# Two blocks of the output projection by seven products instead of eight, with the weight sums made during the attention heads

## The chip, the cores and the metric

The kernel runs on one core of a Trainium2 chip. The metric is the device time in microseconds (us) of one execution. Before the change the median of three runs is 1013.32 us, from 1013.02 to 1014.41.

## The reference

The kernel computes one decoder layer over 256 tokens of width 2048. A normalised input goes through one wide projection; from that come a multi-head latent attention (16 heads) and a short gated convolution; both are projected to the model's width, merged by sigmoid gates, and go through one shared output projection and a last normalisation:

```python
h = _rmsnorm(x, pre_norm_g)
proj = jnp.einsum('bsd,de->bse', h, w_in)
...
y_mla = jnp.einsum('bse,ed->bsd', attn, w_o_mla)
...
y_conv = jnp.einsum('bse,ed->bsd', b_gate * conv * jax.nn.silu(z_conv), w_o_conv)
merged = jax.nn.sigmoid(g_mla) * y_mla + jax.nn.sigmoid(g_conv) * y_conv
out = jnp.einsum('bsd,de->bse', merged, w_out)
x = x + _rmsnorm(out, post_norm_g)
```

All of it is float32. The change concerns `out = merged @ w_out`, with `merged` of 256x2048 and `w_out` of 2048x2048.

## The kernel before

**Products.** A float32 matrix is split into a high part (rounded to the matmul's type) and a low part (the rest), and a product is three matmuls: high by high, low by high, high by low. ACT makes the high part and DVE the low part (`split_act`, L265 and L266). Weights come in *units* of 128x2048 numbers, 1 MB, each loaded by SP into a `raw` buffer of three and split by halves of 1024 columns into `whi` and `wlo`, of which there are five buffers each; so a split waits until PE has let go of the fifth half before it. `plan` lists the units in their order; `take(i)` hands unit i to PE and makes sure that the loads are three units and the splits one unit ahead. A unit stands for 512 features of the contraction and 512 columns. For all 256 tokens (two row blocks, t = 0 and 1) it takes 4 x 2 x 3 = 24 matmuls of 128x512.

**Stages.** After the latent projections 16 heads follow. Head h has four units of a convolution weight (tile `cv`, `channels`), and between them its scores (`sc`, `sw`, made by `score`), the softmax, and the queries and keys of the next group of two heads (`group_a`, whose results are `qn_hi`, `qn_lo` and `kn`; `made[h]` says in which head). `score(h + 1, later=True)` puts a group's first scores right behind the last `cv` matmuls of the head before. In most heads DVE and ACT also make forms of the input (`make_forms`, one step at each `next(form_steps)`, three steps a head), which go out to DRAM through ACT's queue and come back later. Then come the two big projections (tiles `sq` and `sX`, `sY`, `sZ`), which already use the sets of seven products over 2x2 blocks, and then the output stage.

**Output stage.** `merged` stands transposed in four tiles `m_both0` to `m_both3` of 512 features each, with high and low parts, split from `turned_m` (L266 and L265). `w_out` has four blocks c of 512 columns, by four units k. Before the change all four blocks are plain products, 16 units, in the order of `out_order`; each block and row block has a PSUM bank, is squared and summed on ACT (`out_block`, tile `junk`), multiplied with the gain on DVE (`og`, L1503), and finished by `finish` (row block 0) and `finish_by_two` (row block 1): inverse root, scaling and addition of the residual `xr` (L1519), and the stores.

**Order.** The order of PE and of whatever is wrapped in `tc.keep_in_program_order` is that of the program. Everything else is put in order by a scheduler before the kernel is built, which orders each engine's instructions by a timeline of its own. So an added instruction on DVE can change where its neighbours stand. On the chip each engine runs its list in that order, and an instruction that waits holds what is behind it on its engine.

Of the kernel before, what the change touches and what calls it, by code (L numbers as in the profile page):

```python
# [18 lines left out]
P = 128  # L19
# [63 lines left out]
def tile_layer(ctx: ExitStack, tc: tile.TileContext, xw, w0, xb, x, pos, pvec, post_g, wc, wz, wcv, wkr, wqk, wqr, wv, cwr, wsq, out):  # L83
# [61 lines left out]
    out_order = [(0, 0), (0, 1), (1, 0), (1, 1), (0, 2), (1, 2), (0, 3), (1, 3)]  # L145
    out_order += [(c, k) for c in (2, 3) for k in range(4)]
    u_out = {ck: add(wsq[4, ck[0], ck[1]]) for ck in out_order}

    raws, splits, early = {}, {}, {}
    done = {"raw": 0, "split": 0, "end": u_first[1] + 1}  # L150

    def load_raw(i):
        ap, w = plan[i]
        t = early.get(i)
        if t is None:
            t = wpool.tile([P, UNIT], F32, name=f"raw{i}", tag="raw", bufs=3)
        if i == 0:
            pieces = [(S, XW, w0), (XW, 2 * XW, xb[0])]
        elif i in (1, 2):

            pieces = [(j * XW, (j + 1) * XW, xb[2 * i - 1 + j]) for j in range(2)]
        elif i in u_first:
            pieces = []
        else:
            pieces = [(0, w, ap)]
        for a, b, piece in pieces:
            d = nc.sync.dma_start(out=t[:, a:b], in_=piece)
            if i >= u_first[0]:
                tc.keep_in_program_order(d)
        raws[i] = t  # L170
        if i == u_qa[5]:
            tc.keep_in_program_order(nc.sync.dma_start(out=tables_pi, in_=pos))
        if i == u_ckv[1]:
            tc.keep_in_program_order(nc.sync.dma_start(out=x_tok, in_=x))

    def split_unit(i):
# [22 lines left out]
        for h in range(0, w, HALF):  # L199
            n = min(HALF, w - h)  # L200
            if u_out[3, 0] <= i < u_out[3, 3]:
# [6 lines left out]
            split_act(hi[:, :n], lo[:, :n], t[:, h : h + n], i in (u_head[0][1], *u_first, *u_d[0][2][:2]), i in (u_grp["r", 0], u_grp["v", 0], u_head[0][0]))  # L208
            parts.append((hi, lo))
# [13 lines left out]
    def take(i):  # L223
        ahead(i)
        return pieces(splits.pop(i))
# [695 lines left out]

    form, sums = {}, {}
# [8 lines left out]
    form_steps = make_forms()  # L931
# [14 lines left out]
    def turned_unit(far, both, first, tag=None, queue=nc.sync):  # L946
# [4 lines left out]
        def load():  # L951
            name = f"turned_{both.name}{first}"
            if tag:
# [14 lines left out]
        return [[load if i == 0 else None, split(i), None, None] for i in range(len(far))]  # L968
# [25 lines left out]
    for h in range(H):  # L994
# [48 lines left out]
        if h < H - 2:  # L1043
            next(form_steps)
        if v and at == 0 or h == H - 1:
# [22 lines left out]
        if h < H - 2:  # L1068
            next(form_steps)
        channels(h, 2)  # L1070
        if h < H - 2:
            next(form_steps)
        if h == H - 1:
# [51 lines left out]
    LAST = ("f5", "f6", "rb0", "rc0", "rc1", "rb1")  # L1125
# [249 lines left out]
    m_load = [turned_unit(far_m[a:b], m_b, a, tag, nc.gpsimd) for a, b, tag in ((0, 2, "rc0"), (2, 3, "rc1"), (3, 4, "rb1"))]  # L1375
# [91 lines left out]

    m_load[1][0][0]()
# [11 lines left out]
    pss = [[bank(f"out{c}_{t}") for t in range(NT)] for c in range(2)]  # L1480
    for i, (c, kk) in enumerate(out_order[:4]):
        w = take(u_out[c, kk])
        if i == 0:
            last_m[0]()
        elif i == 2:
            m_load[1][0][1]()
        out_products(pss[c], w, kk)
    main.close()


    op = ctx.enter_context(tc.tile_pool(name="op", bufs=1))
    xr = op.tile([P, NT, D], F32, name="xr")
    og = op.tile([P, NT, D], F32, name="og")
    gb = op.tile([P, D], F32, name="gb")
    nc.scalar.dma_start(out=gb[:, :], in_=post_g.to_broadcast([P, D]))

    def out_block(c, t, ps):
# [5 lines left out]
        og_now = nc.vector.tensor_tensor(og[:, t, cs], ps[:, :], gb[:, cs], op=ALU.mult)  # L1503
        if c == 3:
            tc.keep_in_program_order(og_now)
# [50 lines left out]
    for i, (c, kk) in enumerate(out_order[4:6]):  # L1556
        w = take(u_out[c, kk])
        if i == 0:
            last_m[1]()
        out_products(pss[c], w, kk)  # L1560
    tc.keep_in_program_order(nc.sync.dma_start(out=xr[:, :, :], in_=x))
    for c in range(3):
        if c == 2:
            pss.append([bank(f"out{c}_{t}") for t in range(NT)])
        for kk in range(4) if c == 2 else (3,):
            out_products(pss[c], take(u_out[c, kk]), kk)
        for t in range(NT):
            out_block(c, t, pss[c][t])
    nc.vector.reduce_sum(part[:, :], ssq[:, :, :3], axis=mybir.AxisListType.X)
    nc.vector.tensor_scalar(part[:, :], part[:, :], 1.0 / D, EPS, op0=ALU.mult, op1=ALU.add)  # L1570
    pss = [bank(f"out3_{t}") for t in range(NT)]
    for t in range(NT):
        for kk in range(4):
            if t == 0:
                last.append(take(u_out[3, kk]))
            out_products(pss, last[kk], kk, (t,))
        ps = out_block(3, t, pss[t])
# [91 lines left out]
```

## Time and profile before

| what | value |
|---|---|
| median of three runs | 1013.32 us |
| the profiled execution | 1013.55 us |
| its span, first to last instruction | 1011.8 us |
| granted TensorE clock, mean | 0.998 |
| ACT busy / POOL busy | 58% / 17% |
| output stage, first to last of its matmuls | 916.35 to 1003.39 us |
| mean DMA rate over the span | 259 GB/s |

The engines are PE (matmul), PEld (its weight loads), DVE (vector), ACT (scalar), POOL and SP (which here only issues DMAs). The page gives for each the busy time and its share of the span; the chain of work goes back from the last instruction to what released each step; the waits list how long an engine stood idle and on whom it waited. In a timeline a row is start, duration, engine, line, operation, tiles written and read, and in brackets the idle time ahead of it with what ended it. Grouped rows end in the number of instructions, their total and their mean in ns, and the idle time before them. DMA rows give queue, count, size and the median time from issue to landing.

### The profile page before, as it was taken

The numbers are of one execution on the slowest core, as the hardware profiler recorded it, in microseconds if no ns is written. First come the engines' busy times: TensorE is split into PE (matmuls) and PEld (weight loads), VectorE is DVE, ScalarE is ACT, GpSimd is POOL, SyncE is SP. The second block draws the span as 40 slices with busy tenths as digits, with TensorE's granted clock in tenths as the row PEclk, the third lists the DMA queues.
The fourth block names the chain that finished last, engine by engine and source line by source line (L and its number), as shares of the span: only waits on it lengthen the run. The fifth ranks groups of instructions, "written<-read, shape, count | busy, mean of one in ns | idle before, by whom it ended". The sixth has DMA issues, their size and how long they took to land.

```text
span 1011.8 us, 12983 instructions
## 1 busy us (share of the span) xinstructions
PE 1004.2 (99%) x4552; PEld 835.4 (83%) x4552; DVE 811.4 (80%) x1111; ACT 586.3 (58%) x838; POOL 170.7 (17%) x311
## 2 busy tenths in 40 slices
PE   9999999999999999999999999999999999999997
PEld 7888888888888888888888888888888888888886
DVE  7588878868888689877797889898989779997562
ACT  7675656556556456555565465565675664674541
POOL 4620411113211223212133110000000001003000
PEclk9999999999999999999999999999999999999999
DMA  8785768568786668866689779897599989639742
GB/s 338 282 291 183 260 201 304 197 214 276 234 303 232 228 229 283 272 219 232 216 264 338 292 306 291 344 375 218 187 333 296 305 321 260 239 127 322 289 166 84
DMA packets 54369, 261.84 MB, mean 259 GB/s; under 512 B 8768, under 2 KB 13504, under 8 KB 29216
## 3 DMA queue, kind: packets, MB, share of 16 engines
q1 hardware_dynamic: 37728, 214.35, 57.7%
q0 software_dynamic: 12256, 38.13, 14.0%
q10 hardware_dynamic: 4320, 8.54, 2.4%
q8 instruction: 35, 0.57, 0.2%
q14 instruction: 30, 0.25, 0.1%
HBM read 234.80 MB, written 22.02 MB: 254 GB/s over the span
## 4 chain that ended last, share of the span: by engine, by line
PE 98%; DMA 1%; DVE 0%; ACT 0%; SPq 0%; issue 0%
PE cv L88 34%; PE sq L88 17%; PE sX L88 9%; PE z L88 9%; PE out L88 9%; PE sZ L88 4%; PE kn L88 2%; PE qn L88 2%; PE vv L88 2%; PE sY L88 2%; PE ckv L88 2%; PE qa L88 2%; PE qr L88 1%; PE o L88 1%; PE sw L88 1%; DMA raw<-xb_dram 1%
## 5 line engine op out<-in xcount | busy, mean ns | idle before, releaser
L265 ACT ACTIVATE whi<-raw 128x1024 fp32r<-128x1024 f32 (+1 forms) x302 | 306.1, 1028 | 236.7 <-PE cv L88 103.9
L266 DVE TENSOR_TENSOR wlo<-raw,whi 128x1024 fp32r<-128x1024 f32 (+1 forms) x300 | 352.7, 1188 | 101.2 <-ACT whi L265 74.6
L88 PE MATMUL cv<-whi,x_both 128*128 128x512 f32 x1024 | 319.8, 389 | 0.0
L88 PEld LDWEIGHTS cv<-whi,x_both 128*128 128x128 f32 x1024 | 192.3, 188 | 39.5
L88 PE MATMUL cv<-wlo,x_both 128*128 128x512 f32 x512 | 199.5, 390 | 0.0
L88 PEld LDWEIGHTS cv<-wlo,x_both 128*128 128x128 f32 x512 | 96.2, 188 | 19.4
L266 DVE TENSOR_TENSOR slo_V<-b,shi_V 128x1024 fp32r<-128x1024 f32 x60 | 71.5, 1218 | 15.9 <-PE sq L88 8.5
L265 ACT ACTIVATE shi_V<-b 128x1024 fp32r<-128x1024 f32 x60 | 61.5, 1053 | 39.2 <-PE sq L88 21.2
L88 PE MATMUL z<-whi,x_both 128*128 128x512 f32 x256 | 80.0, 389 | 0.0
L366 POOL DMA_DIRECT2D far<-via x64 | 35.4, 559 | 227.2 <-DVE via L358 217.2
L88 PE MATMUL sq<-whi,at_both 128*128 128x512 f32 x256 | 60.6, 389 | 0.0
L88 PE MATMUL sq<-whi,cv_both 128*128 128x512 f32 x256 | 60.6, 389 | 0.0
L88 PEld LDWEIGHTS sq<-whi,cv_both 128*128 128x128 f32 x256 | 48.0, 188 | 10.0
L88 PEld LDWEIGHTS sq<-whi,at_both 128*128 128x128 f32 x256 | 48.0, 188 | 10.0
L88 PEld LDWEIGHTS z<-whi,x_both 128*128 128x128 f32 x256 | 48.1, 188 | 9.9
L88 PE MATMUL z<-wlo,x_both 128*128 128x512 f32 x128 | 49.8, 389 | 0.0
L88 PE MATMUL out<-whi,m_both 128*128 128x512 f32 x208 | 49.4, 389 | 0.0
L88 PE MATMUL sX<-shi_V,form 128*128 128x512 f32 x192 | 47.4, 389 | 0.0
L88 PEld LDWEIGHTS out<-whi,m_both 128*128 128x128 f32 x208 | 39.0, 188 | 8.1
L88 PEld LDWEIGHTS sX<-shi_V,form 128*128 128x128 f32 x192 | 36.0, 188 | 7.5
L265 ACT ACTIVATE shi_Q<-b 128x1024 fp32r<-128x1024 f32 x28 | 28.8, 1052 | 21.5 <-PE sq L88 19.1
L1263 POOL DMA_DIRECT2D b<-wsq_dram x8 | 7.0, 869 | 193.4 <-DVE b L1272 76.8
(304 smaller groups left out, 1568.7 us busy)
## 6 DMA issues: line engine op xcount, KB each, us to landing
raw<-wcv_dram SPq DMA_DIRECT2D x64, 1024.0 KB, 6.2
raw<-wsq_dram SPq DMA_DIRECT2D x48, 1024.0 KB, 7.2
b<-wsq_dram SPq DMA_DIRECT2D x26, 1024.0 KB, 5.7
raw<-wz_dram SPq DMA_DIRECT2D x16, 1024.0 KB, 4.9
raw<-wqk_dram SPq DMA_DIRECT2D x8, 1024.0 KB, 6.8
b<-wsq_dram POOLq DMA_DIRECT2D x8, 1024.0 KB, 11.0
far_form<-form ACTq DMA_DIRECT2D x28, 256.0 KB, 3.3
form<-far_form SPq DMA_DIRECT2D x7, 1024.0 KB, 13.8
```

Of the source, the lines that this page charges most:

```text
L88: return tc.keep_in_program_order(nc.tensor.matmul(*a, **kw))
L265: a = nc.scalar.activation(hi, src, AF.Copy)
L266: b = nc.vector.tensor_tensor(lo, src, hi.bitcast(F32), op=ALU.subtract)
L366: tc.keep_in_program_order(queue.dma_start(out=f[i], in_=m))
L1263: tc.keep_in_program_order(nc.gpsimd.dma_start(out=dst[:, :], in_=wsq[n, c + b, k], accum_op=ALU.add))
```

## The change

Blocks 0 and 3 of the output stay plain. Blocks 1 and 2 are made together: both row blocks of tokens by both halves of the contraction by both blocks of columns are a 2x2 by 2x2 product of blocks, done as seven block products (Q1, V5, V6, V7, V3, V4, Q2) instead of eight. A block product takes one row block of tokens (128) by 1024 features, which is two units of 12 matmuls each. Four of the seven need a sum of weights, and four need a *form* of `merged`, a sum or difference of its blocks.

- **Weight sums.** `make_sums` makes V5, V7, V6 and V4 of the units of blocks 1 and 2: 16 DVE additions of 128x1024, with 16 loads of 512 KB on SP and 16 stores of 512 KB on ACT's queue to `far_sum` in DRAM. They use tiles `at_f` and `cv_f`, whose second halves lie free in the first eight heads. One step is taken at each call of `sums_next(h)`, which stands behind each `next(form_steps)`; seven of the 24 calls, listed in it, do nothing. Only three of the sets need no sum of weights and take their units straight from `wsq`.
- **Forms of merged.** In the output stage `m_form_of` makes V7, V5, V6 and V3: two DVE operations of 128x512 into `m_sums`, a high part on ACT and a low part on DVE over 128x1024. V6 has a negative sign and takes a three-operand instruction for its low part.
- **Banks.** The seven products use three PSUM banks: X for Q1, then V6 on top of it, then V7, then V4; Z for V5, then V3; Y for Q2. In between, the state of a bank is taken out by ACT (`copied`: a from X, c from Z, b from X) and a later one is added by DVE (`added`).
- **Loads.** There are 18 units instead of 16, the splits of all of them are kept in program order, and the loads run five units ahead instead of three. Units of V5, V7 and V4 use a tile `spare` that has room for two and shares its place with `xr`; so the load of `xr` moves to the end of SP's list.
- **The end.** Block 3 has its first two units early in the stage; of its last two, both units of row block 0 come first and then those of row block 1. Before, all four units of row block 1 came behind all four of row block 0.

```diff
+    SUMS = ("V5", "V6", "V7", "V4")
+    far_sum = {(n, u): dram.tile([P, UNIT], F32, name=f"far_sum{n}_{u}") for n in SUMS for u in range(2)}
+    set_raw = {"Q1": (1, 0), "V3": (2, 2), "Q2": (1, 2)}
+    out_order = [(0, 0), (0, 1), (3, 0), ("Q1", 0), ("Q1", 1), (0, 2), ("V5", 0), ("V5", 1), (0, 3), ("V6", 0), ("V6", 1), (3, 1)]
+    out_order += [(n, u) for n in ("V7", "V3", "V4", "Q2") for u in range(2)] + [(3, 2), (3, 3)]
+    in_spare = {u_i: n % 2 for n, u_i in enumerate((6, 7, 12, 13, 16, 17))}
...
-        ahead(i)
+        ahead(i, raw=5 if i >= u_out[0, 0] else 3)
...
+    def make_sums():
+        keep = tc.keep_in_program_order
+        area = [f[:, 4 * i : 4 * i + 4, :].rearrange("p k s -> p (k s)") for f in (at_f, cv_f) for i in (2, 3)]
+        a, b, c, d = area
...
+        bring(0, (0, 1))
+        bring(0, (2,))
+        yield
+        for i in range(4):
+            bring(i, (3,))
+            plus(a, a, b)
+            yield
+            plus(b, b, c)
+            put(i, (1,))
+            yield
+            plus(c, a, c)
+            put(i, (0,))
+            if i < 3:
+                bring(i + 1, (0, 1))
+            yield
+            plus(d, c, d)
+            put(i, (2, 3))
+            if i < 3:
+                bring(i + 1, (2,))
+            yield
...
+    def sums_next(h):
+        q = sum_calls[0] % 3
+        sum_calls[0] += 1
+        if (h, q) not in ((0, 0), (1, 1), (1, 2), (2, 0), (5, 1), (5, 2), (6, 0)):
+            next(sum_steps)
...
+    def m_form_of(n):
+        for j in range(2):
+            if n == "V7":
+                m_sum(0, j, m_raw(j, 0), m_raw(j, 1), ALU.subtract)
+            elif n == "V5":
+                m_sum(0, j, m_raw(2 + j, 1), m_raw(j, 1), ALU.subtract)
+            elif n == "V6":
+                m_sum(1, j, m_part_of(0, j), m_raw(j, 0), ALU.add)
+            else:
+                m_sum(1, j, m_part_of(1, j), m_raw(2 + j, 0), ALU.subtract)
+        m_whole(n, n in ("V6", "V3"), -1.0 if n == "V6" else 1.0)
...
+    then((0, 0), last_m[0])
+    then((0, 1), form_of("V7"))
+    then((3, 0))
+    then(("Q1", 0))
+    then(("Q1", 1), lambda: m_load[1][0][1](True))
+    then((0, 2), form_of("V5"))
+    then(("V5", 0), lambda: last_m[1](True))
+    then(("V5", 1))
+    then((0, 3), lambda: copied("a", "X", "d"), form_of("V6"))
+    then(("V6", 0), lambda: copied("c", "Z", "a"))
+    then(("V6", 1), lambda: out_block(0, 0, pss[0][0]))
+    then((3, 1), lambda: out_block(0, 1, pss[0][1]))
+    then(("V7", 0), lambda: copied("b", "X", "b"), form_of("V3"))
+    then(("V7", 1))
+    then(("V3", 0))
+    then(("V3", 1), lambda: added("c", "X"))
+    then(("V4", 0), lambda: out_block(2, 1, res["c"], -1.0))
+    then(("V4", 1), lambda: added("b", "Z"), get_xr)
+    then(("Q2", 0), lambda: out_block(2, 0, res["b"], -1.0))
+    then(("Q2", 1), lambda: out_block(1, 1, set_bank["X"]))
```

What `then(n, *steps)` adds to `take` stands in the program behind the splits of the *next* unit, since `take(n)` has already asked for these.

The first place where the order moves is on DVE between heads 5 and 6. `wlo56` is the last `cv` unit of head 5, `cv5` its result, `kn3` and `qn3` are the keys and queries of heads 6 and 7 in PSUM, and each is joined to an `f`, from which `kn` and `qn_lo` are made. Before:

```order
L266 TENSOR_TENSOR wlo56_0_2785<-raw56_2698,whi56_0_2784 128x1024
L266 TENSOR_TENSOR qn_lo_2646<-f_2656,qn_hi_2645 128x256
L266 TENSOR_TENSOR qn_lo_2646<-f_2662,qn_hi_2645 128x256
L434 TENSOR_TENSOR f_2686<-kn3_0_2668,half_2687 128x256
L434 TENSOR_TENSOR f_2692<-kn3_1_2669,half_2693 128x256
L806 SCALAR_TENSOR_TENSOR cv_f_110<-cv5_0_2499,r_both_97,cv_f_110 128x512
L266 TENSOR_TENSOR kn_2647<-f_2686,kn_2647 128x256
L266 TENSOR_TENSOR kn_2647<-f_2692,kn_2647 128x256
L266 TENSOR_TENSOR wlo56_1024_2789<-raw56_2698,whi56_1024_2788 128x1024
L806 SCALAR_TENSOR_TENSOR cv_f_110<-cv5_1_2500,r_both_97,cv_f_110 128x512
L898 TENSOR_TENSOR form12_1_2817<-x_area_1009,form12_1_2817 128x2x128
```

And with the change:

```order
L281 TENSOR_TENSOR wlo56_0_2828<-raw56_2741,whi56_0_2827 128x1024
L281 TENSOR_TENSOR qn_lo_2689<-f_2699,qn_hi_2688 128x256
L449 TENSOR_TENSOR f_2705<-qn3_1_2669,half_2706 128x256
L821 SCALAR_TENSOR_TENSOR cv_f_118<-cv5_0_2538,r_both_105,cv_f_118 128x512
L449 TENSOR_TENSOR f_2729<-kn3_0_2711,half_2730 128x256
L281 TENSOR_TENSOR wlo56_1024_2832<-raw56_2741,whi56_1024_2831 128x1024
L821 SCALAR_TENSOR_TENSOR cv_f_118<-cv5_1_2539,r_both_105,cv_f_118 128x512
L281 TENSOR_TENSOR qn_lo_2689<-f_2705,qn_hi_2688 128x256
L913 TENSOR_TENSOR form12_1_2860<-x_area_1017,form12_1_2860 128x2x128
L906 TENSOR_TENSOR form_sum0_1018<-x_area_1017 128x256
L281 TENSOR_TENSOR kn_2690<-f_2729,kn_2690 128x256
```

The first `kn`, that of head 6, stood ahead of `wlo56_1024` and is now the fifth row behind it; the second, of head 7, comes later still. On ACT the same piece of the program now reads as follows, where before `kn` stood ahead of the second `whi56`:

```order
L280 ACTIVATE whi56_0_2827<-raw56_2741 128x1024
L280 ACTIVATE qn_hi_2688<-f_2699 128x256
L448 ACTIVATE half_2730<-kn3_0_2711 128x256
L280 ACTIVATE whi56_1024_2831<-raw56_2741 128x1024
L280 ACTIVATE qn_hi_2688<-f_2705 128x256
L448 ACTIVATE half_2736<-kn3_1_2712 128x256
L918 DMA far_form22_661<-form22_1_2655 128x512
L911 ACTIVATE form12_1_2860<-x_area_1017 128x2x128
L280 ACTIVATE kn_2690<-f_2729 128x256
```

The third place is DVE in the second half of the output stage, with the change. `wlo160` is V7's second unit, 161 and 162 are V3, 163 and 164 V4; `oc` is what `added("c", "X")` adds to, and `out_setX` is bank X:

```order
L281 TENSOR_TENSOR wlo160_0_8746<-spare159_8618,whi160_0_8745 128x1024
L281 TENSOR_TENSOR wlo160_1024_8750<-spare159_8618,whi160_1024_8749 128x1024
L1565 TENSOR_TENSOR m_sums_8370<-m_sums_8370,turned_m23_8361 128x512 x2
L1574 TENSOR_TENSOR m_formV3_8379<-m_sums_8370,m_formV3_8379 128x8x128
L281 TENSOR_TENSOR wlo161_0_8773<-raw161_8681,whi161_0_8772 128x1024
L281 TENSOR_TENSOR wlo161_1024_8777<-raw161_8681,whi161_1024_8776 128x1024
L281 TENSOR_TENSOR wlo162_0_8795<-raw162_8706,whi162_0_8794 128x1024
L281 TENSOR_TENSOR wlo162_1024_8799<-raw162_8706,whi162_1024_8798 128x1024
L281 TENSOR_TENSOR wlo163_0_8817<-spare163_8743,whi163_0_8816 128x1024
L281 TENSOR_TENSOR wlo163_1024_8821<-spare163_8743,whi163_1024_8820 128x1024
L1690 TENSOR_TENSOR oc_8667<-oc_8667,out_setX_8490 128x512
```

Before, this part of the stage had on DVE only the splits `wlo` and, after each block, two `og`. Now a form stands between the splits, and an addition that reads bank X stands behind six splits.

More of the change, by code (lines that the diff above doesn't have):

```diff
@@ L966, in split @@
             return go
-        return [[load if i == 0 else None, split(i), None, None] for i in range(len(far))]
+        return [[load if i == 0 else None, split(i), None, None, box] for i in range(len(far))]
     def split_turned(src, both, t, keep=False):
@@ L1069, in tile_layer @@
             next(form_steps)
+            sums_next(h)
         channels(h, 2)
@@ L1478, in out_products @@
         ])
[L1480 to L1487, printed above, removed]
+    pss = {c: [bank(f"out{c}_{t}") for t in range(NT)] for c in (0, 3)}
+    m_raw = lambda blk, t: by_rows((m_01[0] if blk < 2 else pair_23)[:, (blk % 2) * 1024 + t * 512 :][:, :512], 4)
+    m_form = {n: spool.tile([P, KH, 2, P], F32R, name=f"m_form{n}", tag=tag, bufs=1) for n, tag in (("V5", "f5"), ("V6", "f6"), ("V7", "rb0"))}
@@ L1554, in finish_by_two @@
         store(t, 1536, 2048, og[:, t, cs])
[L1556 to L1568, printed above, removed]
+    res = {}
@@ new lines, in copied, with added, then @@
+    def copied(name, b, tag):
+        res[name] = wide(f"o{name}", tag)
+        tc.keep_in_program_order(nc.scalar.activation(res[name][:, :], set_bank[b][:, :], AF.Copy))
+    def added(name, b):
+        tc.keep_in_program_order(nc.vector.tensor_tensor(res[name][:, :], res[name][:, :], set_bank[b][:, :], op=ALU.add))
+    def then(n, *steps):
+        made = list(map(lambda f: f, steps))
+        c, k = n
+        w = take(u_out[n])
+        for f in made:
+            f()
+        if c in BANKS:
+            set_products(n, w)
+        else:
+            out_products(pss[c], w, k)
```

126 lines of the change are left out of this document (103 added, 23 removed).

## The prediction

> **What bounds the kernel now.** I read the page's busy shares and its chain of work first, then the waits of PE.
>
> ```profile
> PE 1004.2 (99%) x4552; PEld 835.4 (83%) x4552; DVE 811.4 (80%) x1111; ACT 586.3 (58%) x838; POOL 170.7 (17%) x311
> PE 98%; DMA 1%; DVE 0%; ACT 0%; SPq 0%; issue 0%
> PE fin L88 <- ACT dg L1541: 0.9, 1, 0.9
> PE idle L88 <- PEq L1657: 0.8, 1, 0.8
> PE qa L88 <- ACT whi L265: 0.6, 2, 0.3
> ```
>
> PE is busy for 1004.2 us, carries 98% of the chain, and the three rows of its waits add up to 2.3 us. So a matmul taken out is time taken out, and whatever makes PE wait is time put in: there is no slack on PE to absorb either. DVE at 80% looks free on average, so the windows are next, around heads 4 to 6 and over the output stage:
>
> ```profile
> 240.00:260.00 20.00, 20.00 (x93) 16.64 (x92) 19.79 (x34) 11.60 (x20) 7.51 (x14) 1.00 0.74 251
> 250.00:275.00 25.00, 25.00 (x123) 21.14 (x122) 21.33 (x39) 15.06 (x27) 6.36 (x12) 1.00 0.74 251
> 916.35:1003.39 87.04, 87.04 (x385) 72.07 (x384) 47.14 (x53) 35.77 (x47) 7.37 (x14) 1.00 0.59 214
> ```
>
> The columns are the stretch, its length, then PE, PEld, DVE, ACT and POOL busy, the granted clock, the DMA share and GB/s. Between 240 and 260 DVE works 19.79 of 20 us: work added there must push other work back. In the output stage it works 47.14 of 87.04 us: room in sum, though not everywhere. The granted clock is 1.00 in each. The profiled execution took 1013.55 us for a span of 1011.8, and lies 0.23 us above the median of 1013.32.
>
> **What it removes.** Two output blocks cost 192 matmuls before (8 units of 24); the seven products cost 14 units of 12, so 168. That is 24 fewer, or one unit:
>
> ```profile
> 916.35 3.79 PE L88 MATMUL out<-whi,m_both 128*128 128x512 f32 x16
> 919.98 1.98 PE L88 MATMUL out<-wlo,m_both 128*128 128x512 f32 x8
> 921.79 3.79 PE L88 MATMUL out<-whi,m_both 128*128 128x512 f32 x16
> ```
>
> A unit of 24 starts at 916.35 and the next at 921.79: 5.44 us, 0.2267 us a matmul. **Gain: −5.44 us**, and a unit of 12 takes 2.72 us. Shapes and tensor types stay, so the rate does.
>
> **What it adds in the heads.** Sixteen weight sums on DVE, 16 loads of 512 KB on SP, 16 stores of 512 KB on ACT's queue. The nearest row for a sum is the addition over the same 128x1024:
>
> ```profile
> L884 DVE TENSOR_TENSOR x_area<-x_area,r_x 128x1024 f32<-128x1024 f32 x4 | 4.9, 1218 | 0.0
> L265 ACT ACTIVATE whi<-raw 128x1024 fp32r<-128x1024 f32 x282 | 294.0, 1057 | 233.0 <-PE cv L88 103.9 <-PE z L88 31.6 <-PE out L88 24.4
> raw<-wcv_dram SPq DMA_DIRECT2D x26, 1024.0 KB, 6.1
> ...
> far_form<-form ACTq DMA_DIRECT2D x28, 256.0 KB, 3.3
> ```
>
> At 1.22 us each (1.14 from start to start in a run of them) 16 sums are 18 to 20 us of DVE over eight heads. On PE they cost nothing where DVE's idle time takes them. Where it does not, they delay a tile that PE needs. Reading the order of instructions of before and after head by head, the tiles that PE takes from DVE keep their place, or keep a margin of several us, but for one place: the first `kn` of head 6, between heads 5 and 6. These are the rows of before there:
>
> ```profile
> 274.26 0.28 PE L88 MATMUL sc<-kn,qn_hi 128*128 128x256 f32 x1
> 273.10 1.06 ACT L265 ACTIVATE whi<-raw 128x1024 fp32r<-128x1024 f32 x1 [0.95 <-PE cv L88]
> 271.74 0.75 DVE L806 SCALAR_TENSOR_TENSOR cv_f<-cv,r_both,cv_f 128x512 f32<-128x512 f32 x1
> 272.41 0.75 DVE L266 TENSOR_TENSOR kn<-f,kn 128x256 fp32r<-128x256 f32 x2
> 274.19 1.22 DVE L266 TENSOR_TENSOR wlo<-raw,whi 128x1024 fp32r<-128x1024 f32 x1 [1.03 <-ACT whi L265]
> 275.34 0.74 DVE L806 SCALAR_TENSOR_TENSOR cv_f<-cv,r_both,cv_f 128x512 f32<-128x512 f32 x1
> 276.00 0.41 DVE L898 TENSOR_TENSOR form<-x_area,form 128x256 fp32r<-128x256 f32 x1
> 276.33 0.42 DVE L891 TENSOR_TENSOR form_sum<-x_area 128x256 f32<-128x256 f32 x1
> ```
>
> The score of head 6 starts on PE at 274.26; `kn` is done at 273.16, 1.1 us ahead. After the change three sums stand on DVE ahead of this place in the full stretch, and `kn` stands behind `wlo56_1024`, `cv_f`, a `qn_lo`, `form12` and `form_sum0`; on ACT its first half stands behind `whi56_1024`. That `whi` cannot move up: it waits until 273.10 for PE to let go of its buffer. So `wlo56_1024` starts at 274.19 as now, `cv_f` at 275.34, `qn_lo` at 276.00 (a third of a us, as the rows of that size are spaced), `form12` at 276.34, `form_sum0` at 276.67, and `kn` runs from 277.0 to 277.4. The score starts at about 277.46 instead of 274.26: **+3.2 us**. The bounds are 0 (`kn` ready in time after all) and 4.5 (if DVE comes to `wlo56_1024` a sum of 1.2 us late); I take 3.2, since `whi56_1024` hangs on PE alone. After the wait DVE and ACT have caught up, so it is paid once.
>
> The trace shows the granted clock at 1.00 wherever PE is fed and holds no wait of over 0.9 us, so no run here shows what follows on a longer one. [...]
>
> The transfers: DMA ran at 0.74 in these stretches, and 16 MB more are spread over eight heads. A `raw` load lands in 6.1 us there, and what ends the waits of its high half on ACT is PE letting go of buffers (103.9, 31.6 and 24.4 of 233.0 us), not the load: it has been there for a while. The loads of the next sums stand between these on SP, and hold back what is behind them until the store from the same slot has landed; a 256 KB store on ACT's queue takes 3.3 us, so some 5 us here. I put the transfers and this queue at 0, since a `raw` is asked for two to three units of 5.44 us ahead, and bound them by 2 us.
>
> **What it adds in the output stage.** There DVE makes four forms of the merged rows, each of two sums over 128x512 and a low half over 128x1024, with ACT's high half between. The prices:
>
> ```profile
> L266 DVE TENSOR_TENSOR wlo<-raw,whi 128x1024 fp32r<-128x1024 f32 x282 | 340.8, 1220 | 101.1 <-ACT whi L265 74.6 <-PE out L88 19.3 <-PE sY L88 1.8
> L1503 DVE TENSOR_TENSOR og<-out,gb 128x512 f32<-128x512 f32 x7 | 4.8, 685 | 10.0 <-ACT junk L1500 9.9
> L1519 DVE SCALAR_TENSOR_TENSOR og<-og,frr,xr 128x512 f32<-128x512 f32 x5 | 3.6, 748 | 0.0
> 927.05 2.36 DVE L266 TENSOR_TENSOR wlo<-raw,whi 128x1024 fp32r<-128x1024 f32 x2 [3.08 <-PE out L88]
> ```
>
> In a run, a 128x1024 operation is spaced 1.14 us and a 128x512 one 0.6 (two `wlo` take 2.36 in all). From ACT's start of a high half to DVE's start of the low one it is 1.09 above (273.10 to 274.19), with the hand-over to ACT 1.2. So a form costs DVE 1.2 + 1.2 + 1.14 = 3.5 us, of which 1.2 is waiting, since the splits behind it are now kept in program order. A set unit needs 2.28 us of splits in 2.72 us of PE: DVE has only 0.44 us a unit to make up what a form took.
>
> *V6's form.* Count from the start of Q1's first unit. `wlo152_1024` waits for a buffer until 2.54 and ends at 3.68; then come both `m_both2` (4.9), two splits (7.2), V5's form (10.7), two splits (13.0), both `m_both3` (14.2), four splits (18.8), V6's sums (20.0), ACT's high half (21.2) and the low half (22.4). PE has passed Q1 (5.44), block 0 (10.88), V5 (16.32) and block 0 again (21.76), and V6's second matmul wants the low half at 21.99: **+0.45 us**. This low half carries a sign and is a three-operand form that the trace has only at 128x512; between 1.22 (the plain one) and 1.50 (twice 0.748) I take the former, so the bounds are 0.4 and 1.0. V5's form is ready at 10.7 and wanted at 11.1.
>
> *V4 behind `added c`.* Count from the start of unit (3,1). `wlo160_1024` gets its buffer at 5.26, as at 927.05 against the unit's start of 921.79, and ends at 6.40; V3's form ends at 9.94, six splits at 16.8, and then the addition of `oc`, 0.65, at 17.45. It reads bank X, on which V4 accumulates; PE comes there at 5.44 + 4 × 2.72 = 16.32. **+1.2 us**, bounds 0 and 2 (one split more or less ahead of it). Behind this addition stand the splits of V4's second unit, which then have their 2.72 us.
>
> *The end.* These rows show it now:
>
> ```profile
> 993.49 0.69 DVE L1503 TENSOR_TENSOR og<-out,gb 128x512 f32<-128x512 f32 x1 [9.92 <-ACT junk L1500]
> 995.30 2.87 DVE L1519 SCALAR_TENSOR_TENSOR og<-og,frr,xr 128x256 f32<-128x256 f32 x5
> 1003.39 1.02 PE L88 MATMUL fin<-xr,ident 128*128 128x256 f32 x4
> xr<-x_dram SPq DMA_DIRECT2D x1, 2048.0 KB, 12.0
> ```
>
> Row block 0's finishing runs to 998.17, some 5.6 us past its last matmul; after the change 5.44 us of matmuls stand behind that instead of 10.9, so it ends as PE does and is out of the way before row block 1 needs DVE. `xr` now comes in behind the last spare load, at about 20 on the count of V4, lands 12 later and is wanted at about 35. The tail from 1003.39 to 1011.8 stays: 0, bounds −0.5 and +2.
>
> **The sum.** 1013.55 − 5.44 + 3.2 + 1.2 + 0.45 = 1012.96 for an execution like the profiled one; less 0.23 it is **1012.8 us**, no change that can be told.
>
> **The rivals.**
> - *All hidden but the output stage's waits.* If `kn` comes in time, or DVE's idle time takes the sums as it takes them elsewhere, the 3.2 go: 1009.6 us; with nothing waited for at all, 1007.9. For it: PE has only 2.3 us of waits with DVE just as full now. Against it: the order puts `kn` behind a `wlo` whose high half cannot start before 273.10. Chance 0.19.
> - *The spare load ends V4's wait, on the slower side.* V4's raws share a tile with V7's, so their load starts only when `wlo160_1024` is done, at 6.4 on the count above, and its split is due at 13.5: it decides from a landing of 7.1 us, and above 9.7 the kernel is slower by more than 0.2%.
>
> ```profile
> raw<-wsq_dram SPq DMA_DIRECT2D x16, 1024.0 KB, 4.8
> raw<-wsq_dram SPq DMA_DIRECT2D x48, 1024.0 KB, 7.2
> b<-wsq_dram POOLq DMA_DIRECT2D x8, 1024.0 KB, 11.0
> ```
>
> The first row is this stage alone and speaks against it, the second is the whole kernel, the third the slowest queue. At 11.0 the wait is 1.2 + 3.9 and the time 1016.7 us. Chance 0.13.
> - *A longer wait trips the clock.* If the wait for `kn` makes the granted clock fall for some us, each us at half rate loses half a us. [...] From the rows alone it lies between 0 and the 3.2 again, 1016.0. Chance 0.08, most of it still within 0.2%.
> - *A second late tile in the heads.* A sum, or a load held up by the added transfers, eats up a margin elsewhere: one more wait of 1 to 3 us gives 1013.8 to 1015.8. For it: DVE's full stretches; against it: the margins that I read there are 4 to 6 us. Chance 0.08.
>
> **How the numbers follow.** My forecast has 0.52, with its own range of 1011.5 to 1014.3 from the bounds of its small terms. A measurement of this kernel tells 0.2% (2.0 us) from no change. Faster, below 1011.3, are the first rival and the forecast's lower edge: 0.22. Slower, above 1015.3, are the second rival (its chance is meant for landings above 9.7) and the worse ends of the last two: 0.19. The rest, 0.59, is no change. To hold 8 in 10, the range reaches over most of the first rival and the milder half of the second: 1009.4 to 1016.2.
>
> **What would show it.** The matmul count falls by 24 and the output stage lasts some 83.3 us instead of 87.04. PE's waits hold a row of 3.2 us for `kn` on DVE near 277, one of about 1.2 for `oc` and one under 1 for V6's form, and the clock stays 1.00 behind 277. If the first is missing, the first rival is right; if the second names a `whi` that waits for its load, the second is. The forecast falls if PE waits for an engine in another head, or if the last matmuls stand more than 9 us ahead of the end.

## The result, and the profile after

The changed kernel takes 1018.48 us (median of 4 runs, 1017.19 to 1019.28) against 1013.39 us before: a ratio of 1.0051 with a 95% interval of 1.0039 to 1.0064. So it is slower by 5.1 us, by more than the 0.2% that can be told. The forecast was 1012.8 us, with a range from 1009.4 to 1016.2. The profiled execution took 1017.19 us, for a span of 1015.4.

The page of the changed kernel, busy shares and chain of work:

```profile
PE 1001.3 (99%) x4528; PEld 832.1 (82%) x4528; DVE 852.3 (84%) x1154; ACT 602.4 (59%) x857; POOL 170.8 (17%) x311
PE 91%; DVE 4%; DMA 2%; issue 1%; ACT 1%; ACTq 0%; DVEq 0%
```

PE has 24 matmuls fewer, as the change says, but it is busy only 2.9 us less instead of 5.4, and 9% of the chain is off PE, against 2% before. The waits of PE name the places:

```profile
PE sc L88 <- DVE kn L281: 5.1, 1, 5.1
PE out_setX L88 <- DVE oc L1690: 1.1, 1, 1.1
PE fin L88 <- ACT dg L1668: 0.9, 1, 0.9
PE idle L88 <- PEq L1820: 0.8, 1, 0.8
PE qa L88 <- ACT whi L280: 0.6, 1, 0.6
PE out_setX L88 <- DVE m_formV L1576: 0.3, 1, 0.3
```

The three new rows are those of the forecast: `kn`, `oc` and V6's form. The last two have about the size that was forecast (1.2 and 0.45); the wait for `kn` is 5.1 us instead of 3.2. Its place in the timeline of the changed kernel, between heads 5 and 6 (with the three weight sums, L956, that stand ahead of it), and the first matmul of the output stage and of the tail:

```profile
249.98 1.22 DVE L956 TENSOR_TENSOR at_f<-at_f 128x1024 f32<-128x1024 f32 x1
254.41 1.22 DVE L956 TENSOR_TENSOR at_f<-at_f,cv_f 128x1024 f32<-128x1024 f32 x1
259.79 1.18 DVE L956 TENSOR_TENSOR cv_f<-at_f,cv_f 128x1024 f32<-128x1024 f32 x1
260.89 1.21 DVE L281 TENSOR_TENSOR wlo<-raw,whi 128x1024 fp32r<-128x1024 f32 x1
262.13 0.33 SPq L182 DMA_DIRECT2D raw<-wcv_dram  x1
271.81 1.06 ACT L280 ACTIVATE whi<-raw 128x1024 fp32r<-128x1024 f32 x1 [4.08 <-DMA raw<-wcv_dram]
272.90 1.22 DVE L281 TENSOR_TENSOR wlo<-raw,whi 128x1024 fp32r<-128x1024 f32 x1 [3.09 <-ACT whi L280]
273.34 1.05 ACT L280 ACTIVATE whi<-raw 128x1024 fp32r<-128x1024 f32 x1
273.45 0.39 PE L88 MATMUL cv<-whi,x_both 128*128 128x512 f32 x1
275.70 1.21 DVE L281 TENSOR_TENSOR wlo<-raw,whi 128x1024 fp32r<-128x1024 f32 x1
278.50 0.42 DVE L281 TENSOR_TENSOR kn<-f,kn 128x256 fp32r<-128x256 f32 x1
278.97 0.58 PE L88 MATMUL sc<-kn,qn_hi 128*128 128x256 f32 x1 [5.13 <-DVE kn L281]
923.43 3.79 PE L88 MATMUL out<-whi,m_both 128*128 128x512 f32 x16
1007.11 1.02 PE L88 MATMUL fin<-xr,ident 128*128 128x256 f32 x4
```

The same three steps of unit 56 before, the split that frees its `raw` buffer, its load on SP and its first high half:

```profile
257.56 1.22 DVE L266 TENSOR_TENSOR wlo<-raw,whi 128x1024 fp32r<-128x1024 f32 x1
258.80 0.33 SPq L167 DMA_DIRECT2D raw<-wcv_dram  x1
268.04 1.06 ACT L265 ACTIVATE whi<-raw 128x1024 fp32r<-128x1024 f32 x1 [1.03 <-PE kn L88]
```

`wlo56_1024` started at 275.70 and not at 274.19, because unit 56 itself was late: its load left at 262.13 instead of 258.80, right behind a split on DVE that ended 3.3 us later than before, with three sums put ahead of it, and the first high half then waited 4.08 us for the data (271.81 instead of 268.04). The second high half, `whi56_1024`, was nearly on time: 273.34, against 273.10 before. It was DVE that came to it late: it stood idle for 3.09 us until the first high half was there, and then had the first split and four smaller operations to do. From `wlo56_1024` on it goes as forecast: `kn` starts 2.80 us behind it. The first `sc` row shows something else: 0.58 us for a matmul that took 0.28 before. The windows behind the wait tell why:

```profile
276.50:277.00 0.50, 0.00 (x0) 0.00 (x0) 0.50 (x2) 0.50 (x1) 0.50 (x2) 0.85 0.00 0
277.00:277.50 0.50, 0.00 (x0) 0.00 (x0) 0.50 (x2) 0.18 (x1) 0.15 (x1) 0.50 0.53 101
282.00:282.50 0.50, 0.50 (x2) 0.36 (x2) 0.50 (x3) 0.00 (x0) 0.00 (x0) 0.50 1.16 361
283.50:284.00 0.50, 0.50 (x4) 0.42 (x3) 0.08 (x1) 0.39 (x2) 0.00 (x0) 0.82 1.10 287
```

The granted clock, third from the right, falls to 0.50 at about 276.85 (0.85 over that half microsecond) and comes back at about 283.68. While PE waits that costs nothing; from 278.97 on PE runs at half rate for 4.7 us.

So the profiled times add up. The score of head 6 starts 278.97 − 274.26 = 4.71 us later than before. From there to the output stage it takes 644.46 us instead of 642.09, 2.37 more: the half clock. The output stage lasts 83.68 us instead of 87.04, and the tail 8.29 instead of 8.41. In sum 4.71 + 2.37 − 3.36 − 0.12 = +3.60 us, which is the difference of the spans. The median moved by 5.1, since the profiled execution is the fastest of the four. The mean granted clock is 0.995 or 0.996 in all four, against 0.998 or 0.999 in the executions of the kernel before, so each had such a stretch; how long the wait was in the other three is not recorded.

### The profile page after: what moved, and what is told of

The parts are those of the page before. It is cut to its first block, busy times and chain, and to the rows that moved or that the text cites. A ratio compares the mean times of both kernels' runs of the same rounds, so it can differ in the third digit from the quotient of the medians.

```text
span 1015.4 us, 13092 instructions
## 1 busy us (share of the span) xinstructions
PE 1001.3 (99%) x4528; PEld 832.1 (82%) x4528; DVE 852.3 (84%) x1154; ACT 602.4 (59%) x857; POOL 170.8 (17%) x311
## 4 chain that ended last, share of the span: by engine, by line
PE 91%; DVE 4%; DMA 2%; issue 1%; ACT 1%; ACTq 0%; DVEq 0%
PE cv L88 30%; PE sq L88 17%; PE sX L88 9%; PE z L88 8%; PE sZ L88 4%; PE out L88 4%; PE qa L88 2%; PE out_setX L88 2%; PE sY L88 2%; PE ckv L88 2%; PE vv L88 2%; DMA raw<-wcv_dram 2%; PE kn L88 2%; PE qn L88 2%; DVE wlo L281 1%
## 5 line engine op out<-in xcount | busy, mean ns | idle before, releaser
L280 ACT ACTIVATE whi<-raw 128x1024 fp32r<-128x1024 f32 (+1 forms) x306 | 310.0, 1028 | 226.3 <-PE cv L88 100.7
L281 DVE TENSOR_TENSOR wlo<-raw,whi 128x1024 fp32r<-128x1024 f32 (+1 forms) x304 | 357.1, 1188 | 84.0 <-ACT whi L280 72.5
L281 DVE TENSOR_TENSOR slo_Q<-b,shi_Q 128x1024 fp32r<-128x1024 f32 x28 | 33.5, 1220 | 6.2 <-PE sq L88 5.1
L1343 DVE TENSOR_TENSOR b<-b,b 128x2048 f32<-128x2048 f32 x16 | 36.5, 2284 | 0.0
```

The source lines that it names most:

```text
L280: a = nc.scalar.activation(hi, src, AF.Copy)
L281: b = nc.vector.tensor_tensor(lo, src, hi.bitcast(F32), op=ALU.subtract)
L1343: nc.vector.tensor_tensor(t[:, :], t[:, :], raw[plus][:, :], op=ALU.add)
```

## The experiments

Twelve kernels ran, each against the kernel before on the same chip (medians of before: 1013.0, 1013.4 and 1013.1 us for the three groups of four).

**e1: no sums at all.**

```diff
-            u_out[n, k] = add(far_sum[n, k][:, :])
+            u_out[n, k] = add(wsq[4, 1, k])
...
-            next(sum_steps)
+            pass
```

> The weight sums are left out (no loads, additions or stores in the heads; the four sets that need a sum take a raw unit of block 1 instead, so their products are not those of the reference); the output stage is that of the change. My theory: the whole loss sits in the heads, at the wait for kn of head 6. Then no PE wait for kn is left, the clock stays 1.00, oc still costs 1.1 us and V6's form 0.3, and the time is 1013.4 - 5.4 + 1.4 = 1009.4 us. Rival (the output stage itself, or its 18 units, cost more than the profile's two waits say): 1012 us or more.

Measured: 1009.91 us, ratio 0.9965 (0.9951 to 0.9979). PE's waits in the output stage, from the list of that kernel:

```profile
PE out_setX L88 <- DVE oc L1690: 1.1, 1, 1.1
PE out_setX L88 <- DVE m_formV L1576: 0.4, 1, 0.4
```

The wait for `kn` and the half clock are gone (the mean clock is 0.999); the output stage is as it was in the change. The loss lies in the heads. It missed its number by 0.5 us, about what these two waits cost beyond their rows: 2.1 us rather than 1.5 (see e7). The sets that need a sum take other weights here, so this kernel computes something else, with the same matmuls.

**e2: the sums in other steps.**

```diff
-        if (h, q) not in ((0, 0), (1, 1), (1, 2), (2, 0), (5, 1), (5, 2), (6, 0)):
+        if (h, q) not in ((1, 1), (1, 2), (4, 2), (5, 0), (5, 1), (5, 2), (6, 0)):
```

> The sums skip the calls (1,1),(1,2),(4,2),(5,0),(5,1),(5,2),(6,0) instead, so that none is made in the last step of head 4 nor in head 5; on DVE both kn of head 6 stand ahead of wlo56_1024 again, and on SP no sum load stands between raw55 and raw56. My theory (place, not work): no wait for kn, 1009.4 us, at most 1010. Rival (traffic and DVE work of the sums cost time wherever they are): 1012 us or more, with waits elsewhere in the heads.

Measured: 1012.35 us, 0.9994 (0.9985 to 1.0004): in between, so neither was right. In the timeline of PE there is no wait for `kn`, but four new ones, of which these are the largest three:

```profile
93.34 0.49 PE L88 MATMUL cv<-whi,x_both 128*128 128x512 f32 x1 [0.59 <-ACT whi L280]
94.60 0.50 PE L88 MATMUL cv<-wlo,x_both 128*128 128x512 f32 x1 [0.77 <-DVE wlo L281]
305.30 0.50 PE L88 MATMUL cv<-whi,x_both 128*128 128x512 f32 x1 [0.92 <-ACT cv_w L823]
```

The four together are 2.6 us; the profiled span is 3.3 us longer than e1's, the median 2.4. So the sums can make PE wait in other heads too; these waits are only shorter, and the clock stays up (a mean of 0.999 in the profiled execution).

**e3: the two sum loads later.** Only `bring(i + 1, (0, 1))` moves, for i = 2, to the next step.

```diff
-            if i < 3:
-                bring(i + 1, (0, 1))
+            if i != 2:
+                if i < 3:
+                    bring(i + 1, (0, 1))
             yield
             plus(d, c, d)
             put(i, (2, 3))
+            if i == 2:
+                bring(i + 1, (0, 1))
```

> Only the two sum loads that stood on SP ahead of raw56 are made one step later (behind raw58); kn still stands four rows behind wlo56_1024 on DVE. My theory (the order alone costs about 3 us, the late load of raw56 the other 2): PE waits 2.7 to 3.4 us for kn, the clock is not or hardly lowered, 1012.2 to 1013 us. Rival A (the late load is all of it): a wait below 1 us and 1010 us. Rival B (the clock falls after any wait of about 3 us): the same wait, half clock behind it, 1014.5 us. Rival C (the load is harmless): the wait stays at 5 us and the time near 1018.

Measured: 1013.89 us (1012.47 to 1015.91), 1.0010 (1.0001 to 1.0020); the profiled execution took 1015.26. The load of unit 56, its high half, `kn` and the score in the timeline of that kernel:

```profile
262.21 0.33 SPq L182 DMA_DIRECT2D raw<-wcv_dram  x1
269.92 1.06 ACT L280 ACTIVATE whi<-raw 128x1024 fp32r<-128x1024 f32 x1 [1.99 <-DMA raw<-wcv_dram]
274.61 1.22 DVE L281 TENSOR_TENSOR wlo<-raw,whi 128x1024 fp32r<-128x1024 f32 x1
277.06 0.42 DVE L281 TENSOR_TENSOR kn<-f,kn 128x256 fp32r<-128x256 f32 x1
277.54 0.39 PE L88 MATMUL sc<-kn,qn_hi 128*128 128x256 f32 x1 [3.63 <-DVE kn L281]
```

With no sum load ahead of it on SP, the load left at 262.21, no earlier than in the change (262.13). So it was not held back by its queue but by its buffer. What the two sum loads changed is the landing: without them ahead of it the high half started 7.7 us after the issue instead of 9.7; that they took a share of the transfer engines is likely but not shown. The wait is 1.5 us shorter, a third of a us of which comes from `kn` standing one row higher: `wlo56_1024` starts at 274.61, 1.09 earlier than in the change and still 0.42 later than before. And the clock:

```profile
278.50:279.00 0.50, 0.50 (x4) 0.41 (x3) 0.50 (x3) 0.16 (x1) 0.50 (x2) 0.90 0.97 410
282.00:282.50 0.50, 0.50 (x3) 0.36 (x3) 0.47 (x3) 0.00 (x0) 0.50 (x2) 0.69 0.59 127
```

A wait of 3.63 us did lower it, from about 278.9 to 282.3, and the stretch from the score to the output stage took 643.80 us, 1.71 more than before. Rival B was right about the mechanism in this execution, and the mean granted clock on record for each execution shows that it was not alone: four of the ten have 0.995 or 0.996, with a median of 1015.5 us, and the other six 0.998 or 0.999, with a median of 1013.5. The 2.0 us between them are about what the half clock costs here, so much of the spread over 3.4 us is that some executions lose it and others don't.

**e4: work for PE in the wait.** Added in `scores`:

```diff
+        if h == 6:
+            busy = x_both.tiles[0][:, 0, :]
+            for _ in range(16):
+                mm(sc[:, :], busy[:, :P], busy, start=True, stop=True)
```

> The change with 16 matmuls of 128x512 added on PE ahead of head 6's score, into the score's own bank, which the score then starts afresh: 3.6 us of work in the time in which PE waits for kn. Everything else keeps its place. My theory (the idle time lowers the clock): kn comes when it came, PE's wait shrinks to some 1.5 us, the clock stays 1.00 behind it, and the time is 2.3 us below that of the change, about 1016 us. Rival (the clock falls for another reason, such as DMA at full share there): half clock still, 1018.5 us.

Measured: 1015.49 us, 1.0022 (1.0013 to 1.0032), 3.0 us less than the change. PE's timeline, and a window behind it:

```profile
273.85 3.79 PE L88 MATMUL sc<-x_both 128*128 128x512 f32 x16
278.28 0.38 PE L88 MATMUL sc<-kn,qn_hi 128*128 128x256 f32 x1 [0.64 <-DVE kn L281]
```

```profile
280.00:282.00 2.00, 2.00 (x10) 1.64 (x9) 1.97 (x7) 0.27 (x1) 0.49 (x1) 1.00 0.98 335
```

16 matmuls of no use make the kernel faster: the clock stays at 1.00 and from the score to the output stage it takes 642.24 us. DMA is as full as in the change (0.98 against 0.93 in this window) and PE waits 0.64 us instead of 5.13, so in these two profiles it is the idle time that goes with the lower clock. Eight of the ten executions have a mean clock of 0.998 or 0.999; the slowest two, 1016.83 and 1017.27 us, have 0.996, so in them it fell all the same. Some 0.7 us of the gain come from `kn` being earlier in this execution than in the change's.

**e5: the change again, e6: the heads alone.** e5 is unaltered. e6 is the kernel before with `make_sums` and its calls, and nothing that reads `far_sum`:

```diff
...
-    form_steps = make_forms()
+    form_steps, sum_steps = make_forms(), make_sums()
...
             next(form_steps)
+            sums_next(h)
```

> The change itself, unaltered, for another profile and more times. My theory (the wait for kn hangs on when raw56 lands, and above some 3.5 us half clock adds its 2.3 us): the times spread over 2 us or more around 1018, while those of before spread over less; in its profile the time above 1013.0 - 5.4 + 1.5 = 1009.1 us equals the wait for kn plus 2 to 2.5 us. Rival (something else varies): a wait of 5.1 us again with another time.

> The kernel before with the weight sums made in the same steps of the heads, and nothing reading them: the output stage is that of before. My theory (heads and output stage add up): the wait for kn is 4 to 6 us with half clock behind it, 1013.0 + 5.1 + 2.3 = 1020.4 us, between 1019 and 1022. Rival (the loss needs the change's output stage): below 1015 us.

Measured: e5 1017.69 us (1017.48 to 1019.13), e6 1021.55 us, 1.0084 (1.0067 to 1.0100). In e5's profile the wait for `kn` is 4.8 us, and PE waits 1.0 us more for `vv_lo` at 222, which the change's first profile had not. The score starts at 279.62, 5.84 us later than in e1 (273.78), and the half clock costs 2.00 behind it (644.09 us to the output stage instead of 642.09): 7.84 together, for spans of 1015.7 and 1007.9. The change's times spread over 2.1 us in the first group and 1.7 in this one. In e6 the wait is 5.9:

```profile
279.47 0.58 PE L88 MATMUL sc<-kn,qn_hi 128*128 128x256 f32 x1 [5.88 <-DVE kn L268]
```

The score starts 5.21 us later than before (279.47 and 274.26). From there to the output stage it takes 2.16 us more than before, and the stage itself 87.04 us as before. 1013.55 + 5.21 + 2.16 = 1020.92, and this execution took 1020.87 us: heads and output stage add up, and the heads alone carry the whole loss.

**e7: the output stage alone, mended.** e1 with two steps moved in the output stage:

```diff
-    then(("V5", 1))
-    then((0, 3), lambda: copied("a", "X", "d"), form_of("V6"))
+    then(("V5", 1), form_of("V6"))
+    then((0, 3), lambda: copied("a", "X", "d"))
...
-    then(("V3", 0))
-    then(("V3", 1), lambda: added("c", "X"))
+    then(("V3", 0), lambda: added("c", "X"))
+    then(("V3", 1))
```

> The sums left out as in the first experiment (the four sets take raw units of block 1, so their products are not those of the reference), and in the output stage the addition of oc two splits earlier and V6's form two splits earlier. My theory (both waits are DVE's order): neither wait is left, 1009.9 - 1.5 = 1008.4 us. Rival (the waits only move to the splits that are now behind): about 1009.9 us.

Measured: 1007.32 us, 0.9942 (0.9927 to 0.9957). As e1, this kernel computes something else with the same matmuls. Neither wait is left, and the output stage lasts 81.63 us: 87.04 − 5.41, the 24 matmuls and nothing else. Against the change's 83.68 the two waits cost 2.05 us, though their rows say 1.45.

**e8 and e12: both mended.** The steps of e7, and the sums with another list:

```diff
-        if (h, q) not in ((0, 0), (1, 1), (1, 2), (2, 0), (5, 1), (5, 2), (6, 0)):
+        if (h, q) not in ((0, 0), (1, 1), (1, 2), (2, 0), (4, 1), (4, 2), (5, 0)):
```

> The whole computation: the change with the output stage of the run before this one in the list, and with the sums skipping (4,1),(4,2),(5,0) instead of (5,1),(5,2),(6,0), the rest of the skipped calls as in the change. The kn of head 6 stands ahead of wlo56_1024 again, and no sum load ahead of raw56. My theory: no wait for kn and none in the output stage; 1008.4 us if the three moved steps meet idle time, up to 1010.5 if they cause waits of 1 to 2 us such as the other set of steps did. Rival (a wait for kn of over 3 us in another form): 1013 us or more.

> The mended kernel e8 unaltered, for a closer interval and a second profile. My theory: 1008 us, no wait of PE over 1 us. Rival (its first times were lucky, kn has 0.4 us to spare): a median of 1009 us or more and a wait for kn.

Measured: 1008.04 us, 0.9956 (0.9939 to 0.9972), and again 1008.02 us, 0.9957 (0.9944 to 0.9969). Both profiles hold no new wait of PE, but single runs reach 1010.2 and 1011.3.

**e9: the order alone.** e8 with unit 56's split and the `kn` of heads 6 and 7 kept in program order, which puts `kn` behind `wlo56_1024` again, with no sum load ahead of unit 56's:

```diff
-            split_act(hi[:, :n], lo[:, :n], t[:, h : h + n], i in (u_head[0][1], *u_first, *u_d[0][2][:2]) or i >= u_out[0, 0], i in (u_grp["r", 0], u_grp["v", 0], u_head[0][0]))
+            split_act(hi[:, :n], lo[:, :n], t[:, h : h + n], i in (u_head[0][1], *u_first, *u_d[0][2][:2], u_head[5][3]) or i >= u_out[0, 0], i in (u_grp["r", 0], u_grp["v", 0], u_head[0][0]))
...
-            split_act(kn[:, 0, j, :], kn[:, 1, j, :], f[:, :])
+            split_act(kn[:, 0, j, :], kn[:, 1, j, :], f[:, :], g == 3)
```

> The mended kernel of the run e8 with one thing put back: the second half of unit 56's split and both kn of head 6's group are pinned in program order, which puts kn of head 6 three rows behind wlo56_1024 on DVE (behind cv_f and a qn_lo) and its high half behind whi56_1024 on ACT; raw56 is still loaded with no sum load ahead of it. My theory (the place in the order costs time of its own): wlo56_1024 starts 0.1 us ahead of where PE could start the score, then 1.15 + 0.66 + 0.33 + 0.42, so a wait of 2.2 to 2.6 us, no half clock, 1008.0 + 2.4 = 1010.4 us. Rival (the order is harmless, the late raw56 was all): a wait below 0.7 us, 1008 to 1008.8 us.

Measured: 1011.96 us, 0.9991 (0.9981 to 1.0000). `wlo56_1024`, PE's wait, and the clock behind it:

```profile
274.50 1.22 DVE L281 TENSOR_TENSOR wlo<-raw,whi 128x1024 fp32r<-128x1024 f32 x1
277.10 0.39 PE L88 MATMUL sc<-kn,qn_hi 128*128 128x256 f32 x1 [2.64 <-DVE kn L281]
```

```profile
279.00:280.00 1.00, 1.00 (x6) 0.78 (x6) 1.00 (x2) 0.00 (x0) 0.99 (x2) 1.00 1.05 238
```

`wlo56_1024` starts just as PE has nothing left to do (274.50 and 274.46). The place in the order costs a wait of 2.64 us by itself, and in this execution it did not lower the clock. The time is 1.5 us above the expected one: PE comes to this place 0.8 us later than in e8, and 0.8 us more go behind it, with a wait of 0.4 for `cv_w` among them. The two pins also moved other instructions. Six of the ten executions, the profiled one not among them, have a mean clock of 0.996 or 0.997; their median, 1012.0 us, is no longer than that of the other four, 1012.3, so the clock is not what makes e9 slower than expected.

**e10 and e11: two more lists.** As e8, with (0,0),(1,1),(2,0),(4,2),(5,0),(5,1),(5,2) left out in e10, and (1,1),(1,2),(2,0),(4,2),(5,0),(5,1),(5,2) in e11.

> As e8, but the sums skip (0,0),(1,1),(2,0),(4,2),(5,0),(5,1),(5,2). Both kn of head 6's group stand ahead of wlo56_1024 and no sum load ahead of raw56. My theory: no wait for kn; 1007.3 to 1008.5 us, unless a step that now lies in heads 1 or 6 makes PE wait by about 1 us as in e2. Rival: no better than e2 less the output stage's 2.1, 1010.2 us.

> As e8, but the sums skip (1,1),(1,2),(2,0),(4,2),(5,0),(5,1),(5,2), so the first one comes a step earlier, in head 0. Theory and rival as for e10: 1007.3 to 1008.5, or about 1009 where the step in head 0 costs the two waits of 0.6 and 0.8 us at 93 to 95 us that e2 showed there.

Measured: e10 1007.26 us (1007.04 to 1007.97), 0.9943 (0.9930 to 0.9955); e11 1009.03 us, 0.9961 (0.9949 to 0.9974), with a wait of 0.8 us for a `wlo` at 94, as e2 had. The window of the change's output stage, then all the waits of PE in e10, and the window of its output stage:

```profile
923.43:1007.11 83.68, 82.23 (x362) 67.42 (x360) 71.50 (x80) 52.66 (x67) 7.35 (x14) 1.00 0.73 290
```

```profile
PE fin L88 <- ACT dg L1668: 0.9, 1, 0.9
PE idle L88 <- PEq L1820: 0.8, 1, 0.8
```

```profile
915.51:997.11 81.60, 81.60 (x362) 67.57 (x360) 71.43 (x80) 52.50 (x67) 7.38 (x14) 1.00 0.75 297
```

e10 computes all that the change computes, with the same work on every engine, and is 5.8 us faster than the kernel before and 10 to 11 faster than the two medians of the change. The 5.8 is a little more than the 5.44 of the 24 matmuls: in the profiles PE comes to head 6 0.9 us earlier than before (273.37 and 274.26), and nearly all of that is there at 14 us already, where nothing is changed and PE had waited 0.6 us for `whi` in two places. In e10 `kn` of head 6 is done 1.4 us before PE wants it, as before the change; in e8 it was 0.4. That may be why e8's times spread and e10's do not; no run shows it.

## Why the prediction was wrong

- **The gain of 5.44 us** was right: the output stage of e7 and e10 is shorter by 5.41 and 5.44 us.
- **The waits in the output stage** were right in place and somewhat small: 1.65 us forecast, 1.45 in the rows, 2.08 in the length of the stage. V6's form cost no more than a plain one (1.23 us).
- **The step that failed** is the size of the wait for `kn`: "I take 3.2, since `whi56_1024` hangs on PE alone". In the prediction's own terms, the score of head 6 was to start 3.2 us later than before; it started 4.71 us later (the row of the wait says 5.13, since PE came to this place earlier than before). The order cost what was forecast: 2.80 us from `wlo56_1024` to `kn`, and in e9 a wait of 2.64 us from three rows instead of five. What did not hold is "`wlo56_1024` starts at 274.19 as now". It started at 275.70, though its high half was nearly on time, because DVE had waited for the first half of unit 56.
- **Behind it stands a term put at nothing**: the transfers "at 0, since a `raw` is asked for two to three units of 5.44 us ahead". Even before the change the load of unit 56 left only 9.2 us ahead of its high half (258.80 and 268.04), less than two units, since it has to wait for its buffer. The three sums delay the split that frees this buffer, so the load leaves 3.3 us later, and with two sum loads ahead of it 9.7 us pass until the high half starts. That makes `wlo56_1024` 1.51 us late; by e3 some 1.1 of it goes with the two sum loads and 0.4 with the late split. These shares come from one profile each, and the wait itself was 5.1 and 4.8 us in two profiles of the same kernel.
- **The clock** then decided the result. A wait of 5.1 us put PE on half clock, for another 2.4 us. This was a rival with a chance of 0.08. The forecast took 3.2 us with bounds up to 4.5 and put nothing down for the clock; that a wait of this length leaves the clock up was not shown, since the kernel before holds no wait of over 0.9 us. In the profiles 2.64 us of waiting (e9) left it at 1.00, 3.63 us (e3) brought a spell at half clock of about 3.4 us and lost 1.71, and 5.13 us (the change) brought one of 6.8, of which PE felt 4.7, and lost 2.37: both losses lie between the 0 and 3.2 of the rival. In the change the clock fell 3.0 us into the wait (273.84 to 276.85). A term whose bounds reach over such a step should have carried the step in its bounds: 4.5 and the 1.7 of e3 together already give 1015.8.
- **In sum**, the profiled execution lies 4.2 us above the 1012.96 that was worked out for it: 1.5 for `kn`, 2.4 for the clock and 0.4 for the output stage, less 0.1 for the tail. (1012.96 less 0.23 is 1012.7, not 1012.8; nothing hangs on it.)
- **The slower rival** that was given 0.13, the spare load of V4, did not come: V4 waited 1.1 us for `oc` and for nothing else. The range ended at 1016.2 because of it and not because of the place that mattered. A second late tile in the heads, given 0.08, shows in one profile of the change and not in the other: the 1.0 us for `vv_lo` in e5.

## What to carry to other kernels

Work that is added to an engine which looks idle on average is priced by what it pushes back, and that is followed through buffers as well as through the order: from a late split to the buffer that it frees, the load that waits for this buffer, and the split that waits for the load (here the load left 3.3 us later, and `wlo56_1024` started 1.51 us later). A wait of PE is not worth its length alone: here 2.64 us (e9) left the clock at 1.00 in the profile, while 3.63 us (e3) had 0.50 behind it and cost another 1.71, so its bounds have to hold the half clock too. Which steps carry such work is a free choice: with the output stage mended, three lists of steps with the same work lay between 1007.3 and 1009.0 us, and without that the change's own list at 1018.5 and e2's at 1012.4.

## What the runs showed of the hardware

The half clock came in spells of 3.4 us (e3, 278.9 to 282.3) and of 6.8 us, twice as long (the change, 276.85 to 283.68; e5, 276.88 to 283.71; e6, 277.05 to 283.88). These ends are worked out from the mean clock of half microseconds, which is 1.00 or 0.50 apart from those in which it changes. The latter in e5 (the first two) and in e6:

```profile
276.50:277.00 0.50, 0.00 (x0) 0.00 (x0) 0.50 (x1) 0.50 (x2) 0.36 (x1) 0.88 0.97 377
283.50:284.00 0.50, 0.50 (x3) 0.36 (x3) 0.50 (x2) 0.00 (x0) 0.00 (x0) 0.79 0.69 217
277.00:277.50 0.50, 0.00 (x0) 0.00 (x0) 0.50 (x2) 0.50 (x1) 0.50 (x2) 0.55 0.00 0
283.50:284.00 0.50, 0.50 (x3) 0.41 (x2) 0.47 (x3) 0.00 (x0) 0.00 (x0) 0.62 0.85 213
```

The clock did not fall at the same point of a wait. In e5 it was 2.1 us after PE's last matmul (274.81), in the change 3.0 (273.84), in e6 3.5 (273.59). In e3 PE stood idle for 3.63 us, was back at work at 277.54, and the clock fell 1.4 us after that. So there PE was at work when the clock fell; what sets that moment no run shows. Nor does any run show why the same kernel has such a spell in some executions and not in others (e3: by the mean clocks on record, in four of ten).

Useless matmuls in a wait can be worth their place: e4's 16, 3.79 us of PE, saved the whole spell in its profile (642.24 us from the score to the output stage, against 644.46 in the change). And a wait of PE can cost more than its row: the two of the output stage have 1.45 us in rows and cost 2.05 to 2.08. These are their rows in the changed kernel:

```profile
961.56 0.39 PE L88 MATMUL out_setX<-whi,m_formV 128*128 128x512 f32 x1
962.29 1.88 PE L88 MATMUL out_setX<-whi,m_formV 128*128 128x512 f32 x7 [0.34 <-DVE m_formV L1576]
985.23 2.09 PE L88 MATMUL out_setX<-whi,m_both 128*128 128x512 f32 x8 [1.11 <-DVE oc L1690]
```

The rest stands in PE's busy time, 82.23 us against 81.60 in e10 for the same 362 matmuls. A row counts the idle time from the end of the matmul ahead, 0.39 us after its start, whereas in a run the next one starts 0.23 us after it: 0.16 us more for each wait. And the first matmul behind a wait takes 0.50 and 0.47 us instead of 0.39. Both together are 0.5 of the 0.6 us.
